# Two DeepNorm hybrid layers on one core: output projection in weight pieces of 512 columns, input projection in four chunks instead of six, modulation mostly in pieces of 512 features

## The chip, the cores and the metric

The kernel runs on one core of a Trainium2 chip. TensorE (PE) multiplies, VectorE (DVE), ScalarE (ACT) and GpSimd (POOL) do the elementwise work, and SyncE's queue (SP) issues all the transfers between HBM and SBUF. What is measured is the time of one execution on the device, in microseconds; a kernel's time is the median of its runs.

## The reference, cut to what matters

Two layers over 1024 latent tokens and 256 context tokens, 1024 features, all in float32. Each layer is

```python
mod = silu(c) @ ada_w + ada_b                     # 6 x 1024 features: shift, scale, gate, twice; modc from c_ctx
z = (x * (1 + sc1) + sh1) @ w_in                  # 1984 columns, split into:
q_lat, kv_lat, k_r, dq, dk, dv, zch               # 384, 256, 64, 256, 256, 256, 512
o_m = attention(q, k, v)                          # 4 heads from q_lat, kv_lat, k_r; rotary positions
o_d = attention(dq, dk, dv)                       # 4 heads of two maps each, the second subtracted; rotary positions
y = concat(o_m, rms_norm(o_d), chunk_mix(gelu(zch))) @ w_o
x = layer_norm(alpha * x + g1 * y)
x = layer_norm(alpha * x + g2 * conv_ffn(x * (1 + sc2) + sh2))
```

The context tokens go through the same with `modc`; they attend to the context alone, and in layer 1 only their keys and values are needed.

## The kernel before

Every product is made from float32r parts: a matrix is split into `hi` and `lo` (`split`, L455: a ScalarE copy and a subtraction by VectorE or GpSimd), and three matmuls per block of 128 features give `ah*bh + ah*bl + al*bh` (`mm3`, L437). All matmuls of `mm` have line L435. A tile of 128 tokens is the stationary operand, and the weights stream.

The program is written in order as tasks, each with the tiles that it reads and writes, and a planner (`Sched`) then issues them oldest first on a model of the engines, with a cost for each task; an `either` task goes to VectorE or GpSimd. The planner's order is fixed when the kernel is built; each engine, SP's queue too, runs its own list in that order. Places are limited: 8 banks for sums (tag `t`), regions of SBUF that hold the larger tiles (tag `S`, handed out in the program's order), 24 places of 512 words (`C`), 12 of 256 (`H`) and 12 of 512 for modulation weights (`M`).

A layer runs in five steps.

- **Input projection** (`in_proj`, `in_chunk`, `in_tile`). The 1984 columns are cut into six chunks, `ZCH`: z 512, dk 256, dv 256, dq 256, kv 320 (256 and the 64 of `k_r`), q 384. For each chunk the weights are loaded in pieces of up to 1280 words (8 blocks of features), split, and then all ten token tiles are multiplied, 24 matmuls a tile and chunk. Layer 1 takes the two context tiles in dk, dv and kv alone. Behind a tile of dk or dq, `post_d` (L917) rotates 256 columns with five VectorE products and a sum and stores them in `zd` in HBM; behind a tile of kv or q, `post_lat` (L857) normalizes, and `transpose_lat` (L887) transposes two tiles at a time (L901).
- **Attention** over 20 blocks of 256 queries (16 in layer 1). Between them stand the modulation pieces (`mod_piece`, L612) as fillers: 16 of layer 0 and 8 of layer 1 in layer 0, 16 in layer 1; eight more are made ahead of everything. A piece is 256 features: the four columns `s4` (both parts of two vectors) are stationary, 16 matmuls stream 256 columns each, `sel` joins the parts, and `fin` adds the bias.
- **Output projection** (`out_begin`, L1272; `out_half`, L1362). The weights come in 32 units of 256 columns, five to a piece of 1280 words, and are all held. A half tile, 512 features, is two groups of 24 matmuls of 256 columns in one bank. Ten tiles in layer 0, eight in layer 1; six of them stand ahead of the attention's last products (`EARLY`). Ahead of it `row_from_col` (L539) makes rows of the gate.
- **Feed-forward**, with 512-column matmuls for latent tokens and 256 for the context.
- **Norms**, and the transposed tokens for the next product (`emit_hT`, L672).

Of the kernel before, what the change touches and what calls it, by code (L numbers as in the profile page):

```python
# [20 lines left out]
P = 128  # L21
# [10 lines left out]
LAST = (2, 3)  # blocks of the hidden features whose down projection is left to the end, by layer  # L32
# attention: what a block of queries is made of, in this order (see attention)
# [3 lines left out]
COMB_END = 2  # blocks at the end whose two maps are joined by VectorE too  # L37
# [11 lines left out]
ZCH = ["z", "dk", "dv", "dq", "kv", "q"]  # L49
ZN = {"z": 512, "dk": 256, "dv": 256, "dq": 256, "kv": 320, "q": 384}  # L50
ZOFF = {"q": 0, "kv": 384, "dq": 704, "dk": 960, "dv": 1216, "z": 1472}
# [17 lines left out]
class Buf:  # L69
    """A tile that gets its place when its first task is issued."""  # L70
# [12 lines left out]
class Region:  # L83
    """A piece of SBUF that holds tiles of one type; it can change its type when it is empty."""
# [34 lines left out]
class Sched:  # L119
    """Issues a sequential program out of order, oldest task first, on a model of the engines.  # L120

    A task names what it reads and writes; what it depends on follows from the order in which the
    tasks are added. Places of tags in `fifo` are handed out in that order, so the program can
    always go on; no task starts more than `window` tasks ahead of the oldest open one."""
# [4 lines left out]
    def __init__(self, make, fifo, window):  # L129
# [7 lines left out]
        self.starved = None  # the task that waits for the next place of a tag in `fifo`  # L137
# [42 lines left out]
    def seat(self, b):  # L180
        """Gives b a place, or returns False."""
# [156 lines left out]
def either(n):  # L338
    return {**dve_t(n), **pool_t(n)}
# [1383 lines left out]
```

## Time and profile before

| | |
|---|---|
| median of 3 runs | 3498.62 us (3498.55 to 3498.67) |
| span of the profiled execution | 3494.7 us |
| TensorE busy | 3337.1 us, 95% |
| VectorE busy | 2528.8 us, 72% |
| ScalarE, GpSimd busy | 1390.8 us, 1103.9 us |
| matmuls | 19,658 |

The profiled execution has no time of its own beside its span, from the first to the last instruction; the median of the runs is 3.9 us above it. A row's "busy" is the time in which the engine worked on something of that row, and "idle before" the time in which it stood before those instructions, with what ended the wait. The input projection of layer 0 runs from about 82 to 286 us, its attention to about 819, its output projection to about 960; in layer 1 the three end at about 2122, 2604 and 2717 us.

### The profile page before, as it was taken

The page shows a single profiled execution, that of the slowest core. Times are in us where ns is not written, and L with a number is a line of the kernel's source. Part 1 is how long each engine was busy: PE and PEld are TensorE (multiplying, and loading weights), DVE is VectorE, ACT ScalarE, POOL GpSimd, SP SyncE. Part 2 cuts the span into 40 slices and gives each one's busy share as a digit, 9 for nine tenths or more (in the row PEclk, how much of TensorE's full clock was granted, in tenths as well). Part 3 has the DMA queues.
Part 4 walks back from the last instruction along what each step waited for, and adds up shares of the span by engine and source line. Part 5 has one row for each costly group of instructions (what it writes and reads, how often), then busy time and mean ns, then how long its engine had stood idle before and what let it go on. Part 6 is the DMA issues. An engine that isn't in the chain of part 4 may idle for free. (4 is left out here: it accounts for less than half of the span.)

```text
span 3494.7 us, 52898 instructions
## 1 busy us (share of the span) xinstructions
PE 3337.1 (95%) x19658; PEld 2916.4 (83%) x19658; DVE 2528.8 (72%) x6761; ACT 1390.8 (40%) x2428; POOL 1103.9 (32%) x665
## 2 busy tenths in 40 slices
PE   7999999998999999999997999999989899999997
PEld 6998888888988888888886898888879688888885
DVE  7467999998757656565679657999988755555557
ACT  5125666663442222222226225666653322222222
POOL 2102555542113311111134202444433433323322
PEclk9999999999999999999998999999999899999998
DMA  6212223223222211111114211222233311111111
GB/s 236 71 37 76 72 74 82 74 87 118 94 95 91 81 41 37 43 37 37 37 67 136 82 45 56 59 66 66 57 106 109 115 49 53 44 49 47 51 43 73
DMA packets 149258, 252.59 MB, mean 72 GB/s; under 512 B 53256, under 2 KB 85256, under 8 KB 149000
## 3 DMA queue, kind: packets, MB, share of 16 engines
q1 hardware_dynamic: 149000, 249.20, 22.1%
q8 instruction: 155, 2.54, 0.3%
q14 instruction: 103, 0.84, 0.1%
HBM read 209.04 MB, written 40.11 MB: 71 GB/s over the span
## 5 line engine op out<-in xcount | busy, mean ns | idle before, releaser
L435 PE MATMUL t<-region 128*128 128x256 f32 (+3 forms) x16336 | 3004.9, 343 | 77.9 <-DVE region L444 39.4
L435 PEld LDWEIGHTS t<-region 128*128 128x128 f32 x16336 | 2578.8, 191 | 440.3 <-DVE region L444 47.3
L444 POOL TENSOR_TENSOR region<-region 128x512 fp32r<-128x512 f32 (+6 forms) x393 | 620.5, 1586 | 1906.6 <-ACT region L447 1250.8
L1524 DVE SCALAR_TENSOR_TENSOR region<-t,conv,region 128x511 f32<-128x511 f32 (+2 forms) x616 | 341.6, 555 | 443.5 <-ACT region L1527 433.8
L1597 DVE TENSOR_TENSOR region<-region,t 128x512 f32<-128x512 f32 x760 | 456.3, 626 | 141.2 <-PE t L435 141.2
L447 ACT ACTIVATE region<-region 128x512 fp32r<-128x512 f32 (+4 forms) x502 | 385.8, 788 | 281.5 <-POOL region L1549 122.6
L1527 ACT ACTIVATE region<-t,conv 128x512 f32<-128x512 f32 (+1 forms) x220 | 161.4, 734 | 795.6 <-PE t L435 787.5
L447 ACT ACTIVATE region<-t 128x512 fp32r<-128x512 f32 (+4 forms) x711 | 321.4, 490 | 350.8 <-PE t L435 209.6
L444 DVE TENSOR_TENSOR region<-region 128x512 fp32r<-128x512 f32 (+7 forms) x361 | 333.8, 934 | 63.9 <-ACT region L447 52.8
L1099 DVE TENSOR_SCALAR_CACHE_REDUCE region<-t 128x512 f32<-128x512 f32 (+1 forms) x600 | 334.7, 585 | 11.6 <-PE t L435 9.5
L1104 ACT ACTIVATE region<-region,q 128x1280 f32<-128x1280 f32 (+1 forms) x216 | 273.5, 1267 | 162.6 <-DVE q L1103 148.4
L444 DVE TENSOR_TENSOR region<-t,region 128x512 fp32r<-128x512 f32 (+1 forms) x529 | 297.1, 597 | 33.7 <-ACT region L447 32.3
L1168 PE MATMUL t<-ident,region 128*128 128x128 f32 x1312 | 179.3, 280 | 19.2 <-DVE region L1141 8.2
L1144 POOL TENSOR_TENSOR region<-region 128x1280 f32<-128x1280 f32 (+1 forms) x68 | 185.5, 2728 | 5.7
L1168 PEld LDWEIGHTS t<-ident,region 128*128 128x128 f32 x1312 | 150.6, 144 | 27.5 <-DVE region L1141 8.6
L1143 POOL TENSOR_SCALAR region<-region,q 128x1280 f32<-128x1280 f32 (+1 forms) x68 | 85.7, 1261 | 228.5 <-DVE q L1138 104.3
L435 PE MATMUL t<-region,s 128*4 128x256 f32 x768 | 117.2, 292 | 12.9 <-ACT region L447 8.0
L1547 ACT ACTIVATE region<-region 128x512 f32<-128x512 f32 (+1 forms) x110 | 64.9, 590 | 150.0 <-DVE region L1524 149.9
L435 PEld LDWEIGHTS t<-region,s 128*4 128x4 f32 x768 | 64.9, 87 | 41.8 <-ACT region L447 8.2
L517 POOL TENSOR_TENSOR region<-region 128x1024 f32<-128x1024 f32 x31 | 76.0, 2461 | 74.9 <-ACT region L513 28.6
L924 DVE TENSOR_TENSOR region<-t,region 128x256 f32<-128x256 f32 x32 | 13.6, 425 | 110.3 <-PE t L435 110.2
L484 DVE SCALAR_TENSOR_TENSOR q<-q 128x1 f32<-128x1 f32 x276 | 82.2, 302 | 5.5
(127 smaller groups left out, 1758.5 us busy)
## 6 DMA issues: line engine op xcount, KB each, us to landing
region<-in_wup SPq DMA_DIRECT2D x88, 512.0 KB, 3.6
region<-in_ada_w SPq DMA_DIRECT2D x160, 256.0 KB, 3.0
region<-in_w_down SPq DMA_DIRECT2D x46, 512.0 KB, 3.7
n<-region SPq DMA_DIRECT2D x36, 512.0 KB, 2.9
region<-n SPq DMA_DIRECT2D x36, 512.0 KB, 4.4
region<-in_ada_w SPq DMA_DIRECT2D x16, 512.0 KB, 6.9
region<-in_w_o SPq DMA_DIRECT2D x12, 640.0 KB, 6.0
zd<-region SPq DMA_DIRECT2D x58, 128.0 KB, 1.7
```

The costliest lines, as they stand in the source:

```text
L435: self.nc.tensor.matmul(ps, a, b, start=start, stop=stop)
L444: eng.tensor_tensor(out=out, in0=full, in1=hi.bitcast(F32), op=ALU.subtract)
L447: self.nc.scalar.activation(out, in_, AF.Copy, **kw)
L484: self.task(t, lambda e: nc.vector.scalar_tensor_tensor(a.t, y.t, y.t, v.t, op0=ALU.mult, op1=ALU.mult), [y, v], [a])
L1099: self.task(dve_t(b - a), lambda e: nc.vector.tensor_scalar(p[:, a:b], ps[:, :b - a], -scale, None, op0=ALU.mult, op1=ALU.min, accum_out=n ...
L1104: self.task(act_t(nk, 0.19), lambda e: nc.scalar.activation(p[:, :nk], p[:, :nk], AF.Exp, bias=m.t, scale=-1.0, accum_out=s.t), [p, m], [p ...
L1143: nc.gpsimd.tensor_scalar(p2[:, :nk], p2[:, :nk], cc.t, 0.0, op0=ALU.mult, op1=ALU.add)
L1144: nc.gpsimd.tensor_tensor(out=p1[:, :nk], in0=p1[:, :nk], in1=p2[:, :nk], op=ALU.add)
L1168: nc.tensor.transpose(ps[:, u, j * P:(j + 1) * P], B[key][j][:, (kt + u) * P:(kt + u + 1) * P], self.ident)
L1524: nc.vector.scalar_tensor_tensor(o, i, x, o, op0=ALU.mult, op1=ALU.add)
L1527: self.task(act_t(n, 0.15), lambda e: nc.scalar.activation(t[:, a:b], u[:, :n], AF.Identity, scale=c[:, 1:2], bias=c[:, 3:4]), [u, "conv"] ...
L1597: self.task(dve_t(n), lambda e, b=b, o=o, c=c, n=n: nc.vector.tensor_tensor(out=b[:, o:o + n], in0=b[:, o:o + n], in1=ps[:, c:c + n], op=A ...
```

## The change

The six chunks of the input projection become four, z 512, d 512 (dk and dv together), kv 512 (256, the 64 of `k_r`, and 192 of dq) and q 448 (384, and the other 64 of dq, the queries of the last head). The two context tiles of layer 1 use only the first 320 columns of kv. `post_d` is called on a part of a bank: for dk on 256 columns, for dq once on 192 and once on 64, each with its five products, its sum and its store. A chunk's weights come in four pieces of 1024 words (896 for q).

The output weights come in 16 pieces of 512 columns (one block of features, one half), six loaded ahead in place of three pieces of 1280, and a half tile is one group of 24 matmuls of 512 columns.

A modulation piece in the attention has 512 features: eight slabs of 512 columns, 16 matmuls of 512 columns, a bank and a column tile of twice the size. There are 12 in layer 0 and 8 in layer 1. The eight pieces ahead of the program stay at 256 features. `prep_Q` reads dq by the part that holds its head. Comments are taken out too, so a line such as L435 is now L436.

```diff
-IN_AHEAD, FF_AHEAD, WO_AHEAD = 2, 1, 3
+IN_AHEAD, FF_AHEAD, WO_AHEAD = 2, 1, 6
...
-ZCH = ["z", "dk", "dv", "dq", "kv", "q"]
-ZN = {"z": 512, "dk": 256, "dv": 256, "dq": 256, "kv": 320, "q": 384}
...
+ZCH = ["z", "d", "kv", "q"]
+ZCOLS = {"z": [(1472, 1984)], "d": [(960, 1472)], "kv": [(384, 704), (704, 896)], "q": [(0, 384), (896, 960)]}
+ZN = {n: sum(b - a for a, b in c) for n, c in ZCOLS.items()}
...
+    def mod_piece(self, l, n, key=0):
+
+        j, h = QUADS[n // 2], n % 2
+        w = [self.weight(self.i["ada_w"][l, j, h, k], 512, self.M, key=key, acq=True) for k in range(KD)]
+        self.mod_part(l, j, 2 * h, 2, [x[0][0] for x in w], [x[1] for x in w], self.C(), key)
+
+    def mod_part(self, l, j, q, c, wk, wb, m4, key):
...
+        N = 256 * c
+        kk = KD // len(wb)
+        ps, pm = self.bank(), self.bank(F32, (P, 2 * c, 2))
+        for h in range(len(wb)):
             def go(e, h=h):
...
+                for k in range(kk * h, kk * (h + 1)):
+                    hi, lo = wk[k]()
+                    a = self.s4[:, k]
+                    self.mm(ps[:4, :N], a, hi, k == 0, False)
+                    self.mm(ps[:4, :N], a, lo, False, k == KD - 1)
+
+            self.task(mm_t(2 * kk, N), go, ["s4"] + wb[h], [ps], key=key, acq=[m4] if h == 0 else ())
...
     def in_tile(self, l, name, t, wk, wb, tabs):
         nc, hT, N = self.nc, self.hT, ZN[name]
+        dq = l == 0 or t >= 2
+        if name == "kv" and not dq:
+            N = 320
...
-                self.mm3(ps[:, :N], (a[0][:, cs], a[1][:, cs]), wk[k](), k == 0, k == KD - 1)
+                self.mm3(ps[:, :N], (a[0][:, cs], a[1][:, cs]), wk[k](0, N), k == 0, k == KD - 1)
...
-        elif name in ("dk", "dq"):
-            self.post_d(l, name, t, ps, dst, tabs["d"])
-        elif name == "dv":
...
+        elif name == "d":
+            dv = self.H()
+            self.post_d("dk", t, ps, 0, 256, 256, dst, tabs["d"])
+            self.task(act_t(256), lambda e: self.copy(dv.t, ps[:, 256:512]), [ps], [dv])
+            self.dma(lambda: self.zd[cs, 512:768], lambda: dv.t, 4 * P * 256, [dv], [("zd", "dv", t)])
         else:
+            a, n, off = (320, 192, 0) if name == "kv" else (384, 64, 192)
+            if dq:
+                self.post_d(f"dq{off}", t, ps, a, n, off, self.C() if n > 64 else self.H(), tabs["d"])
             return self.post_lat(l, name, t, ps, dst, tabs.get("k"))
...
-            self.task({"dve": 0.9}, rope, [ps, dtab], [o])
...
+            self.task({"dve": 0.55 + 1.4e-3 * n}, rope, [ps, dtab], [o])
...
-        units = [5] * 6 + [2]
-        wo = Stream(self, [dict(src=self.i["w_o"][l, j, :, :256 * n], n=256 * n, k=n) for j, n in enumerate(units)], WO_AHEAD)
-        wo.prime(3)
+        wo = Stream(self, [dict(src=self.i["w_o"][l, j], n=512) for j in range(2 * KD)], WO_AHEAD)
+        wo.prime(6)
...
-            for j in range(2):
-                for k in range(KD):
-                    self.mm3(ps[:, j * 256:(j + 1) * 256], y[k](), wk[4 * k + 2 * hh + j](), k == 0, k == KD - 1)
+            for k in range(KD):
+                self.mm3(ps.t, y[k](), wk[2 * k + hh](), k == 0, k == KD - 1)
...
-            ada = [(0, n) for n in range(8, 24)] + [(1, n) for n in range(8)] if l == 0 else [(1, n) for n in range(8, 24)]
+            ada = [(0, n) for n in range(4, 12)] + [(1, n) for n in range(4)] if l == 0 else [(1, n) for n in range(4, 12)]
```

Three places show how the order of the engines moves. A row has the line, the operation, the tiles, the output's shape and the number in a row. The first is TensorE at the end of the input projection of layer 0, before: matmuls of the q chunk (384 columns), the transposes of its results (L901), the queries' transposes of the attention (L1084), and the first modulation pieces (`s_70` is `s4`, `sel_71` is `sel4`).

```order
L435 MATMUL t<-region 128x384 x48
L901 MATMUL t<-ident,region 128x128 x6
L435 MATMUL t<-region 128x384 x48
L901 MATMUL t<-ident,region 128x128 x6
L1084 MATMUL t<-identr,region 128x128 x12
L435 MATMUL t<-region,s_70 4x256 x20
L435 MATMUL t<-sel_71,region 128x2 x2
L901 MATMUL t<-ident,region 128x128 x6
L435 MATMUL t<-region,s_70 4x256 x16
L435 MATMUL t<-sel_71,region 128x2 x2
```

And now, where the q chunk has 448 columns and the three lines are L914, L1098 and L436:

```order
L436 MATMUL t<-region 128x448 x72
L914 MATMUL t<-ident,region 128x128 x6
L436 MATMUL t<-region 128x448 x144
L914 MATMUL t<-ident,region 128x128 x18
L1098 MATMUL t<-identr,region 128x128 x8
L436 MATMUL t<-region,s_70 4x512 x10
L1098 MATMUL t<-identr,region 128x128 x4
L914 MATMUL t<-ident,region 128x128 x6
L436 MATMUL t<-region,s_70 4x512 x8
L436 MATMUL t<-sel_71,region 128x2 x4
```

The transposes that followed each two token tiles now stand in one run of 18 behind the last six tiles, with the queries' transposes and the first modulation products around the rest.

The second is SP's queue in the input projection of layer 0, before: the last loads of the weights of kv and q among the stores of the finished tiles (`yt` of chunk z, `zd` of dk, dv and dq).

```order
L432 DMA region<-in_w_in_q 128x1152
L432 DMA yt<-region 128x256
L432 DMA region<-in_w_in_q 128x1152
L432 DMA yt<-region 128x256
L432 DMA zd<-region 128x256
L432 DMA region<-in_ktab 128x1024
L432 DMA zd<-region 128x256 x2
L432 DMA yt<-region 128x256
L432 DMA zd<-region 128x256 x27
L432 DMA region<-in_w_in_q 128x768
```

And now, where a `zd` store of 256 columns is one of dk or dv, and one of 192 columns belongs to a tile of kv:

```order
L433 DMA region<-in_w_in_q 128x896 x2
L433 DMA zd<-region 128x256 x2
L433 DMA yt<-region 128x256
L433 DMA region<-in_ktab 128x1024
L433 DMA zd<-region 128x256 x2
L433 DMA yt<-region 128x256
L433 DMA zd<-region 128x256 x16
L433 DMA zd<-region 128x192 x2
L433 DMA region<-in_w_in_q 128x896
L433 DMA zd<-region 128x192
L433 DMA region<-in_w_in_q 128x896
L433 DMA zd<-region 128x192 x5
```

The last piece of q stood behind all of the stores of dq; now the last two stand behind the second and the third of the ten stores of the kv tiles.

The third is TensorE toward the end of layer 1's attention, before: the last modulation products, their `sel` product, and what follows; the transposes of the gate (L539) begin 13 rows behind that `sel` row.

```order
L435 MATMUL t<-region 128x256 x5
L1168 MATMUL t<-ident,region 128x128 x20
L435 MATMUL t<-region,s_70 4x256 x4
L435 MATMUL t<-region 128x512 x2
L435 MATMUL t<-region 128x256 x9
L435 MATMUL t<-region 128x512
L435 MATMUL t<-region 128x256 x4
L435 MATMUL t<-sel_71,region 128x2 x2
L1196 MATMUL t<-ident,q 128x128 x2
L435 MATMUL t<-region 128x256 x8
```

And now, the same place in the program, the last modulation piece, with L540 51 rows behind its `sel` row:

```order
L436 MATMUL t<-region,s_70 4x512 x2
L1182 MATMUL t<-ident,region 128x128 x4
L436 MATMUL t<-region 128x256 x12
L436 MATMUL t<-region,s_70 4x512 x4
L436 MATMUL t<-region 128x256 x4
L1182 MATMUL t<-ident,region 128x128 x4
L436 MATMUL t<-region 128x256 x4
L436 MATMUL t<-sel_71,region 128x2 x4
L1182 MATMUL t<-ident,region 128x128 x4
L436 MATMUL t<-sel_81,region 128x64 x2
```

The last modulation piece has moved ahead, away from the attention's last blocks.

## Rows read from the trace of the kernel before

**Rows 1.** The page's first lines: the span, and for each engine its busy time in us, its share of the span and its number of instructions.

```profile
span 3494.7 us, 52898 instructions
...
PE 3337.1 (95%) x19658; PEld 2916.4 (83%) x19658; DVE 2528.8 (72%) x6761; ACT 1390.8 (40%) x2428; POOL 1103.9 (32%) x665
```

**Rows 2.** Groups of TensorE's matmuls by line and shape, over the whole span: line, engine, operation, tiles, stationary operand and output, number; then busy us, mean ns of one (they overlap), and the idle time before them.

```profile
L435 PE MATMUL t<-region 128*128 128x512 f32 x8024 | 1922.5, 396 | 37.9 <-DVE region L444 17.4 <-ACT region L447 16.2 <-POOL region L444 2.2
L435 PE MATMUL t<-region 128*128 128x256 f32 x7256 | 979.4, 287 | 28.5 <-DVE region L444 22.0 <-DVE region L1099 3.8 <-DVE q L1103 0.8
...
L435 PE MATMUL t<-region,s 128*4 128x256 f32 x768 | 117.2, 292 | 12.9 <-ACT region L447 8.0 <-DVE region L444 4.7
L435 PE MATMUL t<-region 128*128 128x384 f32 x432 | 77.9, 338 | 0.0
L435 PE MATMUL t<-region 128*128 128x320 f32 x480 | 72.8, 310 | 0.0
```

**Rows 3.** Two stretches in which TensorE has matmuls of one width alone: 256 columns in the input projection of layer 0, and 512 in the feed-forward part of layer 1. Columns: from:to, us, then busy us (and number) of PE, PEld, DVE, ACT and POOL, the granted clock, the DMA share, GB/s.

```profile
130.00:180.00 50.00, 50.00 (x424) 50.00 (x423) 8.90 (x39) 4.22 (x11) 0.00 (x0) 1.00 0.15 48
...
2800.00:2900.00 100.00, 100.00 (x439) 82.08 (x438) 54.85 (x97) 25.48 (x33) 35.04 (x19) 1.00 0.14 47
```

**Rows 4.** The timeline of TensorE, merged: start us, length us, engine, line, operation, out<-in, number. In this order: modulation and the row after it, chunk z of the input projection, chunk kv, chunk q, and a token tile of the output projection; a stretch is read from its start to the start of the next row.

```profile
35.40 2.90 PE L435 MATMUL t<-region,s 128*4 128x256 f32 x24
38.23 0.60 PE L435 MATMUL t<-sel,region 4*128 4x2 f32 x4
...
41.40 8.47 PE L435 MATMUL t<-region 128*128 128x512 f32 x36
49.71 2.03 PE L435 MATMUL t<-region,s 128*4 128x256 f32 x16
...
221.67 7.27 PE L435 MATMUL t<-region 128*128 128x320 f32 x48
228.77 0.60 PE L901 MATMUL t<-ident,region 128*128 128x128 f32 x4
...
249.97 8.66 PE L435 MATMUL t<-region 128*128 128x384 f32 x48
258.47 0.82 PE L901 MATMUL t<-ident,region 128*128 128x128 f32 x6
...
833.65 11.76 PE L435 MATMUL t<-region 128*128 128x256 f32 x96
845.25 0.60 PE L1321 MATMUL t<-ident,region 128*128 128x128 f32 x4
```

**Rows 5.** Stretches, with the columns of rows 3: chunk kv and chunk q of layer 0, the end of the attention of layer 0, the output projection of layer 0 and of layer 1.

```profile
217.95:240.59 22.64, 22.64 (x161) 22.62 (x160) 20.70 (x123) 12.24 (x34) 2.73 (x1) 1.00 0.07 19
249.97:285.61 35.64, 35.64 (x213) 35.50 (x212) 23.75 (x117) 14.66 (x40) 2.29 (x3) 1.00 0.17 51
750.00:800.00 50.00, 41.31 (x292) 36.85 (x292) 47.22 (x120) 32.55 (x54) 15.97 (x8) 0.93 0.29 93
850.00:900.00 50.00, 50.00 (x421) 50.00 (x420) 41.17 (x169) 13.89 (x19) 3.87 (x3) 1.00 0.36 117
2650.00:2700.00 50.00, 50.00 (x421) 49.86 (x420) 44.86 (x150) 17.13 (x27) 15.52 (x8) 1.00 0.34 118
```

**Rows 6.** Groups of VectorE and ScalarE that follow the input projection, with the columns of rows 2: the rotation's products and sum (L924, L930, L933) in 124 to 217 us, the lower part of a q weight piece (218 to 241 us) and of a transposed block (250 to 286 us), and ScalarE's copies of weight pieces of 1024 and of transposed blocks over the whole span.

```profile
L930 DVE TENSOR_TENSOR region<-t,region 128x64 f32<-128x64 f32 x64 | 9.7, 215 | 0.0
L933 DVE TENSOR_TENSOR region<-region 128x256 f32<-128x256 f32 x15 | 6.4, 425 | 0.5
L924 DVE TENSOR_TENSOR region<-t,region 128x256 f32<-128x256 f32 x15 | 6.4, 425 | 58.0 <-PE t L435 58.0
...
L444 DVE TENSOR_TENSOR region<-region 128x1152 fp32r<-128x1152 f32 x1 | 1.4, 1353 | 0.0
...
L444 DVE TENSOR_TENSOR region<-t,region 128x256 fp32r<-128x256 f32 x11 | 4.0, 417 | 1.5 <-ACT region L447 1.5
...
L447 ACT ACTIVATE region<-region 128x1024 fp32r<-128x1024 f32 x158 | 162.0, 1049 | 29.6 <-PE t L435 8.8 <-DVE region L561 7.2 <-DMA region<-in_ada_w 4.7
L447 ACT ACTIVATE region<-t 128x256 fp32r<-128x256 f32 x193 | 67.1, 380 | 32.7 <-PE t L435 30.7 <-PE t L901 1.2
```

**Rows 7.** Groups of ScalarE and VectorE in 770 to 815 us, the end of layer 0's attention, with the columns of rows 2: both parts of the output weights in pieces of 1280, ScalarE's in pieces of 512, and VectorE's subtraction of 512 from a bank.

```profile
L447 ACT ACTIVATE region<-region 128x1280 fp32r<-128x1280 f32 x6 | 7.7, 1279 | 0.0
L447 ACT ACTIVATE region<-region 128x512 fp32r<-128x512 f32 x2 | 1.3, 627 | 0.3 <-PE t L435 0.3
...
L444 DVE TENSOR_TENSOR region<-t,region 128x512 fp32r<-128x512 f32 x18 | 11.7, 680 | 0.2
L444 DVE TENSOR_TENSOR region<-region 128x1280 fp32r<-128x1280 f32 x3 | 5.9, 1950 | 0.1
```

**Rows 8.** The page's DMA issues: out<-in, queue, operation, number, KB each, median us from issue to landing. The 16 loads of 512 KB are the first modulation pieces.

```profile
region<-in_ada_w SPq DMA_DIRECT2D x160, 256.0 KB, 3.0
...
region<-in_ada_w SPq DMA_DIRECT2D x16, 512.0 KB, 6.9
region<-in_w_o SPq DMA_DIRECT2D x12, 640.0 KB, 6.0
```

**Rows 9.** Waits of TensorE in 280 to 830 us, the attention of layer 0, the longest in total: who waits <- for whom, us in total, times, longest us.

```profile
PE t L435 <- DVE region L444: 13.6, 14, 2.4
PE t L1168 <- DVE region L1141: 4.3, 1, 4.3
```

More of the change, by code (lines that the diff above doesn't have):

```diff
@@ L606, in setup, with mod_load, mod_first @@
         self.n2 = d.tile([SEQ, D], F32, tag="n2", name="n2")
-    def mod_src(self, l, n, h):
-        return self.i["ada_w"][l, QUADS[n // 4], n % 4, h]
-    def mod_piece(self, l, n, key=0, raws=None):
+    def mod_load(self, n, h):
+        return self.load(self.i["ada_0"][QUADS[n // 4], n % 4, h], 1024, self.L)
+    def mod_first(self, n, raws):
+        w = [self.weight(None, 1024, self.L, k=4, raw=raws[h]) for h in range(2)]
+        self.mod_part(0, QUADS[n // 4], n % 4, 1, [f for x in w for f in x[0]], [x[1] for x in w], self.H(), 0)
@@ L613, in mod_piece @@
+    def mod_piece(self, l, n, key=0):
[3 more added lines that the diff above has]
+    def mod_part(self, l, j, q, c, wk, wb, m4, key):
         nc = self.nc
         self.s.what = f"mod{l}"
-        j, q = QUADS[n // 4], n % 4
-        if raws:
-            w = [self.weight(None, 1024, self.L, k=4, raw=raws[h]) for h in range(2)]
-        else:
-            src = [self.mod_src(l, n, h)[:, a:a + 512] for h in range(2) for a in (0, 512)]
-            w = [self.weight(x, 512, self.M, k=2, key=key, acq=True) for x in src]
@@ L634, in sel @@
+        self.task(act_t(N), lambda e: self.copy(m4[:4], ps[:4, :N]), [ps], [m4], key=key)
         def sel(e):
-            for k in range(2):
+            for k in range(2 * c):
                 self.mm(pm[:, k], m4[:4, k * P:(k + 1) * P], self.sel4)
-        self.task({"pe": 0.25}, sel, [m4, "sel4"], [pm], key=key)
-        ks = slice(2 * q, 2 * q + 2)
+        self.task({"pe": 0.25 * c}, sel, [m4, "sel4"], [pm], key=key)
+        ks = slice(2 * q, 2 * (q + c))
         o = self.modv[l][:, j, ks]
-        tok = ("modv", l, j, q)
@@ L643, in fin @@
         def fin(e):
[L644 removed]
+            nc.vector.tensor_tensor(out=o, in0=pm.t, in1=self.adab[l][:, j, ks].unsqueeze(2).to_broadcast([P, 2 * c, 2]), op=ALU.add)
             if j in (1, 4):
                 nc.vector.tensor_scalar(o, o, 1.0, None, op0=ALU.add)
[L648 removed]
+        self.task({"dve": 0.15}, fin, [pm, ("adab", l)], [("modv", l, j, q + x) for x in range(c)], key=key)
@@ L703, in mod @@
             for n in (q, 4 + q):
-                self.mod_piece(0, n, raws=[self.load(self.mod_src(0, n, h), 1024, self.L) for h in range(2)])
+                self.mod_first(n, [self.mod_load(n, h) for h in range(2)])
         mod(0)
@@ L805, in in_chunk @@
         held = []
-        tiles = range(0 if l == 0 or name in ("kv", "dk", "dv") else 2, NT)
+        tiles = range(0 if l == 0 or name in ("kv", "d") else 2, NT)
         for t in (8, 9, 0, 1) if l == 0 and name == "z" else tiles:
@@ L1273, in out_begin @@
         self.s.what = f"wo{l}"
-        units = [5] * 6 + [2]
-        wo = Stream(self, [dict(src=self.i["w_o"][l, j, :, :256 * n], n=256 * n, k=n) for j, n in enumerate(units)], WO_AHEAD)
-        wo.prime(3)
+        wo = Stream(self, [dict(src=self.i["w_o"][l, j], n=512) for j in range(2 * KD)], WO_AHEAD)
+        wo.prime(6)
         self.go = {s: self.row_from_col(lambda s=s: self.modv[l][:, 2, :, s], self.modtok(l, 2)) for s in ((0, 1) if l == 0 else (0,))}
-        w = [wo.get(j) for j in range(7)]
+        w = [wo.get(j) for j in range(2 * KD)]
         self.wo = [f for x in w for f in x[0]], [b for x in w for b in x[1]]
```

54 lines of the change are left out of this document (19 added, 35 removed).

## The prediction

> **What bounds the kernel now.** I read the page's busy shares first. TensorE works 3337.1 of 3494.7 us, VectorE 2528.8 [rows 1]: the time is TensorE's, and only what shortens its queue or fills its 158 us of gaps can count. Next, the matmuls by shape: 8,024 of 512 columns, 7,256 of 256, 768 of 256 for the modulation, 480 of 320, 432 of 384 [rows 2]. The mean durations there overlap, since matmuls are pipelined, so what one costs has to be read as a pitch: stretches with one shape and no gap, time divided by count. A stretch of 256 columns has 424 matmuls in 50.00 us, 117.9 ns each, and one of 512 columns 439 in 100.00 us, 227.8, both at a granted clock of 1.00 [rows 3]. The timeline of TensorE gives the rest as start-to-start differences [rows 4]: modulation 24 in 2.83 us (117.9), the 512-column chunk z 36 in 8.31 us (230.8), 320 columns 48 in 7.10 us (147.9), 384 columns 48 in 8.50 us (177.1), and 256 columns in the output projection 96 in 11.60 us (120.8). The granted clock of these stretches is the upper level, 2.4 GHz, at which 256 columns would stream in 106.7 ns and 512 in 213.3; so each matmul pays 11 to 17 ns beyond its columns. In the same windows the weight-load row is busy 50.00 of 50.00 us at 256 columns and 82.08 of 100.00 at 512 [rows 3]: at the narrow width loads leave no slack.
>
> **The change, part by part.** No column is added or taken away; the same columns go in fewer matmuls. The counts follow from the code: the input projection loses 48 of 120 per full token tile (18 tiles) and 24 of 72 on the two context tiles of layer 1, 912; the output projection loses 24 of 48 per half tile, 36 halves, 864; 40 modulation pieces become 20, and lose 320. Together 2,096.
>
> *Input projection.* Before, a full tile costs 24 x (3 x 117.9 + 147.9 + 177.1) = 24 x 678.7 ns. After, it is 24 x (512 + 512 + 448 columns). For 512 I take 229.4, the middle of 227.8 (feed-forward stretch) and 230.8 (the z chunk, the same operands' shape but with busy loads around it). No row has 448 columns; 384 costs 0.461 ns a column, 512 costs 0.445 to 0.451, so 199 to 207, and I take 204. That is 24 x 662.8, a gain of 0.38 us a tile, 6.9 for 18, and 0.3 for the two context tiles: **7.2 us**, bounds 4.8 (230.8 and 207) and 10.4 (227.8 and 199).
>
> *Output projection.* 48 x 120.8 = 5.80 us a half becomes 24 x 229.4 = 5.51: 0.29 us on 36 halves, **10.5 us**, bounds 9.3 and 11.8 by the two prices of 512. TensorE is busy throughout both stretches, and VectorE 41.17 and 44.86 of 50.00 us [rows 5]; with stages 5% shorter the second comes to about 95% and just keeps pace.
>
> *Modulation.* 2 x 117.9 - 229.4 = 6.4 ns on 320 matmuls, **2.0 us**; a stationary operand of four columns with 512 moving ones stands in no row, so bounds 0 and 5.
>
> *What is added.* The query columns of the differential heads lose their own chunk and are rotated from the banks of the kv and q chunks: two rotations of five VectorE operations for one, and two stores for one. They leave a stretch in which VectorE works 8.90 of 50.00 us [rows 3] for two in which it works 20.70 of 22.64 and 23.75 of 35.64 [rows 5]. One rotation of 256 columns takes 425 + 4 x 215 ns = 1.29 us [rows 6]; with that on top, VectorE needs at most 3.45 + 1.29 = 4.7 us for a kv tile that TensorE now works 5.5 us on, and 2.97 + 1.29 + 0.43 = 4.7 for a q tile of 4.9 plus transposes. Hidden, cost nothing, but with little room; if the cover went, up to 1.3 us on each of 34 tiles. The additional 18 stores go through SP's queue beside work that waits for nothing of theirs.
>
> *The end of the q chunk.* In the order, transposes that stood between the q tiles now stand in one run after the last tile, 18 in layer 0 and 12 in layer 1. Each pair is emptied by a ScalarE copy (380 ns) and a VectorE subtraction (417 ns) [rows 6], slower than TensorE fills them, six transposes in 0.82 us [rows 4]. Nine pairs: 3.8 us against 2.5. I put **2 us lost** for both layers, bounds 0 and 6.
>
> *Output weights.* Sixteen pieces of 512 in place of six of 1280 and one of 512: on ScalarE 16 x 0.63 = 10.0 us for 6 x 1.28 + 0.63 = 8.3, on VectorE 16 x 0.68 = 10.9 for 6 x 1.95 + 0.68 = 12.4 [rows 7]. These lie at the end of the attention, where TensorE waits for VectorE (41.31 against 47.22 of 50.00 us busy [rows 5]), so they count: between -1.5 and +1.7 us a layer, taken as 0. Loads shrink from 640 KB (6.0 us to landing) towards the 256 KB that take 3.0 [rows 8], and six are ahead in place of three: as many bytes, nothing on the path. The modulation's loads stay 160 of 256 KB, with one slab, not two, for each wait of TensorE on a pair of hi and lo parts, and the same number of waits.
>
> *Sum.* 7.2 + 10.5 + 2.0 - 2.0 = 17.7 us. 3494.7 - 17.7 = 3477.0 for the span; the runs' median, 3498.6, lies 3.9 us above the profiled span, so **3481 us**. Its own range, with the bounds not all at one end, is 3472 to 3490.
>
> **The rivals.**
> A. *Width is worth almost nothing.* Per column, 256, 320 and 384 cost 0.461, 0.462 and 0.461 ns [rows 3, 4]: a price by the column, not by the matmul. If the new 512s went by it (236 ns), the input projection and the modulation would gain nothing and the output projection 36 x (5.80 - 24 x 0.236) = 4.8 us: 3494, within 0.2%. The two rows that do have 512 columns (227.8 and 230.8) speak against it, and one of them has the same operands. The Trainium skill comes to the same side in another way (TensorE: Matmul & The Clock Gate, "Back-to-back issue gap"): it gives a gap of N/2.4 + 2.5 ns, so halving the count would save only 2.5 ns a matmul, 5 us in all and about 3493, an estimate by that page. The trace disagrees with its floor: 117.9 ns stand where it has 109.2, and 227.8 to 230.8 where it has 215.8.
>
> B. *The ends of the attention get shorter too.* TensorE waits 13.6 us on VectorE's subtractions in layer 0's attention and after [rows 9], most at its end. In the order of TensorE the last modulation product of layer 1 now stands 51 rows before the first transpose of the residual gate in place of 13, and in layer 0 35 in place of 13, so four or more splits of 0.63 and 0.68 us leave that end. If 5 us a layer go with them: 3471.
>
> C. *Slower: a chunk waits for its weights.* A chunk's weights are now four pieces that must all be there for its first tile, and a load stands behind others in SP's queue and waits for a place that TensorE's earlier chunk gives up. If the last piece is issued later than landing plus splits before its first use, 6.9 us [rows 8] + 1.05 + 1.35 [rows 6] = 9.3 us, TensorE stands for up to that at each of six switches (three in each layer). From three such stalls on (28 us against 17.7) the change loses: 3509. Against it: in the order the last two q loads of layer 0 stand behind two and three of the ten stores of the kv tiles, some seven tiles, 38 us, ahead of use.
>
> **How the numbers follow.** Forecast 0.60; A 0.15; B 0.11; C 0.10; 0.04 for gains that are spread over new small waits, near 3495. Differences under 0.2%, 7 us, are about what a measurement of this kernel cannot tell from none. Faster by more is nearly all of the forecast and B, 0.70; within 0.2% is A, the last case and the forecast's weak end, 0.20; slower is C, 0.10. The range takes in B's 3471 with the bounds' best sum below it, and A, but not C: 3468 to 3497.
>
> **What would show it.** In the profile after: 17,562 matmuls in place of 19,658; a half of the output projection in 5.5 us, 24 at about 229 ns; a run of 512 columns in the d chunk at the same pitch and 448 near 204. C would show as TensorE's gaps ended by ScalarE or VectorE splits of pieces of 1024 at the start of d, kv or q; A as a pitch of 236; a gap of over 5 us behind the last q tile would upset the 2 us there. The forecast fails if VectorE's share in the kv or q chunk reaches its whole and the tile time is then set by it.

## The result, and the profile after

The changed kernel takes 3535.47 us (median of 4 runs, 3535.01 to 3539.42) against 3498.64: a ratio of 1.0109, 95% interval 1.0095 to 1.0123. The forecast was 3481 us. The profiled execution took 3535.01 us with a span of 3533.2. Every ratio in this document is of runs in the chip's faster state; the one run outside it, of e11, took 6577.16 us. First the head of the page of the changed kernel:

```profile
span 3533.2 us, 48850 instructions
...
PE 3343.4 (95%) x17562; PEld 2798.8 (79%) x17562; DVE 2541.3 (72%) x6859; ACT 1386.1 (39%) x2421; POOL 1080.3 (31%) x668
```

The change does what it says: 17,562 matmuls. But TensorE is busy 6.3 us more than in [rows 1] with 2,096 fewer, and 32.2 us longer without work. The timeline of TensorE (columns of rows 4) gives the new pitches: in chunk kv, chunk q, the modulation and a token tile of the output projection.

```profile
205.65 11.14 PE L436 MATMUL t<-region 128*128 128x512 f32 x48
216.63 0.64 PE L914 MATMUL t<-ident,region 128*128 128x128 f32 x4
...
259.80 15.37 PE L436 MATMUL t<-region 128*128 128x448 f32 x74
275.00 1.69 PE L914 MATMUL t<-ident,region 128*128 128x128 f32 x14
...
302.51 2.48 PE L436 MATMUL t<-region,s 128*4 128x512 f32 x10
304.83 1.22 PE L436 MATMUL t<-region 128*128 128x256 f32 x9
...
847.97 11.26 PE L436 MATMUL t<-region 128*128 128x512 f32 x48
859.07 0.60 PE L1334 MATMUL t<-ident,region 128*128 128x128 f32 x4
```

48 in 10.98 us are 228.8 ns (forecast 229.4); 74 in 15.20 are 205.4 (204); 10 in 2.32 are 232; 48 in 11.10 are 231.3. The prices of the sum stand (the last is 0.5 ns above its upper bound), so the loss is elsewhere. Nine stretches show where, with the columns of rows 3 (the second is the length): up to the last product of layer 0's q chunk; from there to the first transposes of probabilities (the junction below); the rest of the attention; output projection; feed-forward; norm and input projection of layer 1 up to its last q product; its attention; its output projection; the rest. The kernel before:

```profile
0.00:285.80 285.80, 264.37 (x1730) 243.83 (x1731) 181.29 (x680) 93.42 (x179) 45.14 (x33) 0.96 0.33 110
285.80:323.40 37.60, 35.88 (x273) 31.16 (x272) 26.01 (x86) 22.16 (x60) 3.22 (x5) 0.95 0.35 104
323.40:819.50 496.10, 466.25 (x3336) 415.24 (x3337) 458.85 (x1379) 330.40 (x643) 251.83 (x161) 0.98 0.27 78
819.50:960.60 141.10, 139.15 (x1127) 136.50 (x1126) 109.86 (x412) 52.79 (x83) 25.32 (x24) 0.99 0.33 107
960.60:1810.60 850.00, 849.98 (x4194) 718.32 (x4193) 528.56 (x922) 230.20 (x344) 177.63 (x94) 1.00 0.16 54
1810.60:2118.20 307.60, 282.96 (x1766) 260.66 (x1765) 227.62 (x848) 109.26 (x210) 85.20 (x62) 0.94 0.27 87
2118.20:2610.50 492.30, 454.62 (x3196) 405.75 (x3195) 443.08 (x1298) 309.20 (x581) 213.26 (x125) 0.97 0.23 69
2610.50:2729.10 118.60, 117.38 (x916) 113.46 (x915) 101.14 (x326) 40.86 (x65) 39.13 (x27) 0.99 0.37 123
2729.10:3494.70 765.60, 726.54 (x3137) 591.54 (x3135) 452.41 (x815) 202.48 (x267) 263.17 (x135) 0.97 0.16 55
```

And the changed kernel:

```profile
0.00:275.20 275.20, 256.79 (x1238) 211.88 (x1239) 175.19 (x702) 92.35 (x176) 46.25 (x41) 0.98 0.33 113
275.20:322.00 46.80, 42.09 (x276) 33.71 (x275) 32.14 (x109) 26.35 (x69) 11.71 (x14) 0.93 0.34 94
322.00:834.10 512.10, 469.87 (x3155) 405.90 (x3154) 468.44 (x1378) 324.76 (x632) 228.91 (x146) 0.97 0.26 75
834.10:986.00 151.90, 138.77 (x647) 113.33 (x645) 110.14 (x415) 52.44 (x83) 22.82 (x22) 0.94 0.30 99
986.00:1842.90 856.90, 856.58 (x4194) 717.61 (x4193) 530.35 (x923) 230.25 (x344) 175.49 (x93) 1.00 0.16 54
1842.90:2156.10 313.20, 282.38 (x1332) 237.02 (x1331) 228.26 (x882) 109.30 (x208) 86.16 (x67) 0.94 0.26 84
2156.10:2644.00 487.90, 452.09 (x3069) 395.03 (x3067) 440.58 (x1311) 307.60 (x578) 209.68 (x127) 0.98 0.25 70
2644.00:2764.90 120.90, 115.20 (x532) 94.49 (x531) 104.38 (x333) 40.85 (x65) 35.40 (x22) 0.96 0.35 120
2764.90:3533.20 768.30, 729.63 (x3137) 589.84 (x3135) 451.77 (x814) 202.18 (x267) 263.88 (x136) 0.97 0.16 55
```

After less before, in this order: -10.6, +9.2, +16.0, +10.8, +6.9, +5.6, -4.4, +2.3, +2.7 us, together 38.5. Three things are to be seen. Layer 0's projection gains more than forecast, and its junction gives nearly all of it back. Some of this is work that changed sides. TensorE's modulation products and transposes of q in the junction, before and then in the changed kernel (columns of rows 2):

```profile
L435 PE MATMUL t<-region,s 128*4 128x256 f32 x48 | 7.6, 318 | 1.5 <-ACT region L447 1.1 <-DVE region L444 0.4
L901 PE MATMUL t<-ident,region 128*128 128x128 f32 x12 | 1.8, 282 | 0.0
```

```profile
L436 PE MATMUL t<-region,s 128*4 128x512 f32 x32 | 9.2, 397 | 2.5 <-DVE region L445 1.8 <-ACT region L448 0.7
L914 PE MATMUL t<-ident,region 128*128 128x128 f32 x24 | 3.3, 278 | 0.3 <-DVE region L445 0.3
```

Twelve transposes have left the stretch ahead of the last q product and stand here, 1.6 us at six in 0.82 us, and 32 modulation products at 232 ns take 1.8 us more than 48 at 118: together some 3.4 of the 9.2 us, an estimate. The rest is 3.0 us more without work for TensorE (4.7, 1.7) and a lower granted clock (0.93, 0.95). Up to the end of the junction the changed kernel is 1.4 us ahead. The rest of the attention loses 16.0 although VectorE and GpSimd together are given about the same work: some of it has moved from GpSimd (251.83 to 228.91) to VectorE (458.85 to 468.44). And the two feed-forward stretches, which the change doesn't touch (4,194 and 3,137 matmuls in both), are 9.6 us longer.

The waits of TensorE (columns of rows 9) in the rest of the attention, and in layer 0's output projection:

```profile
PE t L436 <- DVE region L445: 28.0, 26, 3.4
...
PE t L679 <- ACT region L514: 9.8, 1, 9.8
```

In [rows 9], over a somewhat longer stretch, the first was 13.6. The second is one wait of the transposes behind a norm; windows around it (columns of rows 3) show what follows a wait:

```profile
935.00:940.00 5.00, 0.71 (x6) 0.47 (x4) 4.73 (x15) 1.02 (x2) 1.51 (x2) 1.00 0.01 2
940.00:945.00 5.00, 0.00 (x0) 0.00 (x0) 2.25 (x14) 2.03 (x3) 0.00 (x0) 0.59 0.00 0
945.00:950.00 5.00, 4.32 (x19) 3.92 (x19) 3.26 (x9) 4.37 (x10) 1.50 (x3) 0.50 0.68 212
950.00:955.00 5.00, 3.06 (x6) 1.99 (x7) 4.97 (x11) 1.46 (x3) 1.55 (x2) 0.50 0.85 312
955.00:960.00 5.00, 5.00 (x17) 3.96 (x16) 2.71 (x14) 0.00 (x0) 0.00 (x0) 0.71 0.00 0
```

The granted clock falls to the lower level, 1.2 GHz (0.50), and TensorE is at work again for some ten microseconds before it is back: this wait is paid twice.

### The profile page after: what moved, and what is told of

The parts are those of the page before. It is cut to its first block, busy times and chain, and to the rows that moved or that the text cites. A ratio compares the mean times of both kernels' runs of the same rounds, so it can differ in the third digit from the quotient of the medians.

```text
span 3533.2 us, 48850 instructions
## 1 busy us (share of the span) xinstructions
PE 3343.4 (95%) x17562; PEld 2798.8 (79%) x17562; DVE 2541.3 (72%) x6859; ACT 1386.1 (39%) x2421; POOL 1080.3 (31%) x668
## 5 line engine op out<-in xcount | busy, mean ns | idle before, releaser
L436 PE MATMUL t<-region 128*128 128x512 f32 (+4 forms) x14560 | 2999.9, 364 | 84.8 <-DVE region L445 49.2
L436 PEld LDWEIGHTS t<-region 128*128 128x128 f32 x14560 | 2478.6, 190 | 557.5 <-DVE region L445 61.7
L445 POOL TENSOR_TENSOR region<-region 128x512 fp32r<-128x512 f32 (+4 forms) x376 | 579.1, 1548 | 1787.5 <-ACT region L448 1276.4
L448 ACT ACTIVATE region<-region 128x512 fp32r<-128x512 f32 (+3 forms) x522 | 387.7, 765 | 296.6 <-POOL region L1561 121.8
L448 ACT ACTIVATE region<-t 128x512 fp32r<-128x512 f32 (+5 forms) x684 | 313.1, 499 | 354.7 <-PE t L436 193.4
L445 DVE TENSOR_TENSOR region<-region 128x512 fp32r<-128x512 f32 (+5 forms) x398 | 354.5, 902 | 74.9 <-ACT region L448 55.4
L436 PE MATMUL t<-region,s 128*4 128x512 f32 (+1 forms) x448 | 118.9, 381 | 23.3 <-DVE region L445 12.7
L937 DVE TENSOR_TENSOR region<-t,region 128x256 f32<-128x256 f32 (+2 forms) x48 | 16.1, 336 | 116.4 <-ACT region L448 70.3
L448 ACT ACTIVATE region<-t,q 128x64 f32<-128x64 f32 (+2 forms) x110 | 38.9, 384 | 121.4 <-DVE q L487 110.6
```

The source lines that it names most:

```text
L436: self.nc.tensor.matmul(ps, a, b, start=start, stop=stop)
L445: eng.tensor_tensor(out=out, in0=full, in1=hi.bitcast(F32), op=ALU.subtract)
L448: self.nc.scalar.activation(out, in_, AF.Copy, **kw)
```

## The experiments

Ratios are against the kernel before, run on the same chip.

**One part each** (e1, e2, e3). The hunks of the change for one part alone, in the kernel before:

```diff
-ZCH = ["z", "dk", "dv", "dq", "kv", "q"]                       # e1, with in_tile, post_d, prep_Q
+ZCH = ["z", "d", "kv", "q"]
-        wo = Stream(self, [... 256 * n ... for j, n in enumerate(units)], WO_AHEAD)   # e2, with out_half
+        wo = Stream(self, [dict(src=self.i["w_o"][l, j], n=512) for j in range(2 * KD)], WO_AHEAD)
-    def mod_piece(self, l, n, key=0, raws=None):               # e3, with mod_part and the list ada
+    def mod_piece(self, l, n, key=0):
```

> The kernel before with the input projection in four chunks and nothing else. If the losses belong to the parts that they stand at, this one keeps the gain of layer 0's projection (10.6 us from the first to the last product of the q chunk in the changed kernel), loses about 5 us in the stretch from layer 0's last norm to layer 1's q chunk, and leaves the attention at its time of before: about 3493 us. If any new order of the planner shifts the attention and the ends of the stages, whatever was edited, the attention of layer 0 moves by some 10 to 25 us here too, in either direction, and the total is between 3485 and 3515.

> The kernel before with the output projection in 16 weight pieces of 512 columns and nothing else. If the pieces are the loss (16 pieces of 512 words, two to a region of 1280, hold more places than six of 1280 and one of 512, so loads of the last token tiles come late), the wait of some 10 us for a norm in layer 0's output projection and its drop of the granted clock stand here too, and the time is 3508 to 3515. If the pieces are harmless, the 10.5 us of the prediction show: 3488.

> The kernel before with the modulation of the attention in pieces of 512 features and nothing else. If half as many and twice as long fillers are what costs layer 0's attention its 25 us, the time is about 3520. If they are harmless, 2 us are gained: 3497. If only the shuffled order counts, the attention of both layers moves by 5 to 25 us in either direction.

Measured: e1 3530.62 us, 1.0092 (1.0075 to 1.0108), above what either of its theories allowed; e2 3512.91, 1.0044 (1.0029 to 1.0059); e3 3527.40, 1.0086 (1.0071 to 1.0101). Each part alone loses, together 80 us (before: 3496.96), more than twice what all three lose at once: these can't all be costs that belong to the parts. e3 alone could be read by its theory of the fillers as well as by that of the order; e7 and e8 below decide. e2 has the time that its first theory asked for, but not its wait: layer 0's output projection takes 144.2 us (141.1 before); 6.2 us are in the untouched feed-forward of layer 0, and one wait of 18.0 us for a GpSimd subtraction stands behind layer 1's output projection. The rest of layer 0's attention takes 515.5 us in e3, and in e1:

```profile
320.20:839.70 519.50, 478.23 (x3336) 424.12 (x3337) 466.57 (x1373) 333.41 (x645) 257.54 (x166) 0.96 0.25 75
```

e1 has the same matmuls in this stretch as the kernel before (3,336), and takes 23.4 us longer in it.

**Width alone** (e4). The pieces of before, and so its tasks and its order; only the matmuls are wider:

```diff
-            for j in range(2):
-                for k in range(KD):
-                    self.mm3(ps[:, j * 256:(j + 1) * 256], y[k](), wk[4 * k + 2 * hh + j](), k == 0, k == KD - 1)
+            for k in range(KD):
+                u = 4 * k + 2 * hh
+                if u % 5 < 4:
+                    self.mm3(ps.t, y[k](), wk[u](0, 512), k == 0, k == KD - 1)
+                else:
+                    for j in range(2):
+                        self.mm3(ps[:, j * 256:(j + 1) * 256], y[k](), wk[u + j](), False, False)
```

> The kernel before with its weight pieces of 1280 columns as they are, but matmuls of 512 columns wherever both units of 256 lie in one piece, 13 of 16 of each token tile; tasks, costs, places and loads are those of before, so the planner's order is too. This is the width alone: 864 x 13/16 = 702 matmuls less, 13/16 of 10.5 us gained: 3490. If width is worth almost nothing in the whole, because VectorE or the norms set the pace, 3497 to 3499.

Measured: 3492.56 us, 0.9985 (0.9976 to 0.9995): 4.4 us less (medians), about half of what the prices give. Its two output projections (columns of rows 3; 141.10 and 118.60 us before):

```profile
817.90:955.10 137.20, 133.68 (x736) 114.07 (x735) 109.33 (x413) 52.69 (x83) 25.50 (x24) 1.00 0.33 110
...
2608.40:2726.80 118.40, 114.86 (x605) 96.66 (x604) 101.31 (x326) 40.80 (x65) 39.10 (x27) 0.98 0.36 123
```

Layer 0 gains 3.9, layer 1 nothing: there TensorE works 2.5 us less and stands 2.3 us longer. Of its waits in that stretch 2.2 us are for ScalarE's splits and 0.6 for VectorE's, and VectorE works as long as before (101.31 us, 101.14); which of the two engines holds the stage isn't shown.

**Places** (e5, e6). In the program as built, a matmul's operands lie at one of three offsets within 256 bytes (0, 192 and 224 before, 32, 192 and 224 in the changed kernel), by when a region's first tile came. With these addresses laid beside the trace, 512-column matmuls whose operands and next weights share the offset have another pitch than the others:

```
                 same offset        other
before        6051 at 228.0    1745 at 233.1 ns
after         5131 at 229.0    4397 at 232.9 ns
```

The edit, in the kernel before (e5) and the changed one (e6), moves every large tile to one offset, 224, and leaves each engine's instructions and their order as they were:

```diff
         self.s = Sched(make, ("S",), WINDOW)
+        for r in self.s.regions:
+            sb.tile([P, r.words], F32, tag=r.name, name="region", bufs=1)
```

> The kernel before, all 32 regions claimed at the start, one behind the other, so that every operand of a matmul lies at the same offset of 256 bytes; tasks, order and loads are those of before. In the trace of before 512-column matmuls whose two operands and next weights share that offset have a pitch of 228.0 ns, the others 233.1; 1745 are of the other kind. If the place in memory sets the pitch, they fall to 228 or under, the stretch 2800 to 2900 us has 440 or more matmuls in place of 439, and the time is 3484 to 3492. If the pitch has another cause, 3497 to 3499.

> The changed kernel with its regions claimed in the same way. 4397 of its 512-column matmuls are of the other kind, at 232.9 ns. If places set the pitch, some 25 to 30 us go, most of it in the two feed-forward stretches, the projections and the attention: 3505 to 3512. If not, 3535.

Measured: e5 3488.87 us, 0.9974 (0.9964 to 0.9984); e6 3513.03, 1.0035 (1.0023 to 1.0047), where the change had 1.0109, a little above what was expected. 2900 to 3000 us, feed-forward of layer 1, 512 columns alone (columns of rows 3): the kernel before, the changed one, e5, e6.

```profile
2900.00:3000.00 100.00, 100.00 (x438) 81.98 (x437) 54.16 (x94) 25.90 (x34) 35.07 (x19) 1.00 0.14 48
```

```profile
2900.00:3000.00 100.00, 100.00 (x435) 81.21 (x434) 53.87 (x94) 25.48 (x33) 34.61 (x19) 1.00 0.15 48
```

```profile
2900.00:3000.00 100.00, 100.00 (x443) 82.81 (x442) 55.73 (x97) 25.85 (x34) 35.66 (x19) 1.00 0.14 48
```

```profile
2900.00:3000.00 100.00, 100.00 (x443) 82.81 (x442) 55.74 (x98) 26.13 (x34) 36.44 (x20) 1.00 0.14 48
```

438, 435, 443 and 443 matmuls: 228.3, 229.9 and twice 225.7 ns, at one clock and with one work. The two feed-forward stretches, 850.0 and 765.6 us before and 856.9 and 768.3 in the changed kernel, take 844.5 and 759.2 in e5 and 845.1 and 757.1 in e6: with places alike nothing of their 9.6 us is left. Places change the pitch, the change had more tiles in unlike places, and that is 0.74% of its time (1.0109 to 1.0035) against 0.26% before: some 17 us of its loss, with an interval of about 0.1% to either side on each of the ratios. The Trainium skill (SBUF — State Buffer, "Who interferes with whom") gives TensorE two independent read ports, for the moving operand and for the weights. That gives no reason for places to matter, and e5 and e6 show that they do. That the offset, and not another property of a place, does it rests on the two classes above, since e5 moved every large tile.

**The same work in another order** (e7, e8). The kernel of e5 with one constant of the planner changed:

```diff
-def dve_t(n, per=1.042e-3, extra=0.0):     # e7
+def dve_t(n, per=1.05e-3, extra=0.0):
-MODKEY = 120                               # e8
+MODKEY = 110
```

> The kernel of e5 with nothing changed but a constant in the planner's model: VectorE's cost of 1.042 ns an element becomes 1.05. The work is the same, instruction for instruction; the order moves from the end of the input projection on. If the kernel's order is one that any reshuffle makes worse, layer 0's attention gets 10 to 25 us longer, with more waits and a lower granted clock, and the time is 10 to 35 us above e5. If losses come from what the edits themselves do (more splits, larger pieces, fewer fillers), it is within 5 us of e5.

> The kernel of e5 with nothing changed but MODKEY, 120 to 110: how far ahead of its place in the program the planner may take a modulation piece. Same work; the order moves in the attentions alone. By the theory of the reshuffled order 5 to 30 us above e5 with the loss in the attentions and behind them; by the theory of the edits' own costs within 5 us of e5.

Measured: e7 3514.72 us, 1.0048 (1.0030 to 1.0066), 25.9 above e5; e8 3510.21, 1.0031 (1.0019 to 1.0042), 21.3 above. The rest of layer 0's attention in e5, e7 and e8:

```profile
324.80:823.80 499.00, 469.46 (x3335) 418.91 (x3336) 458.22 (x1378) 330.68 (x643) 251.84 (x161) 0.98 0.26 77
```

```profile
324.30:845.50 521.20, 477.46 (x3329) 426.99 (x3330) 470.80 (x1381) 331.57 (x646) 243.02 (x155) 0.95 0.25 75
```

```profile
322.00:836.20 514.20, 474.78 (x3330) 422.93 (x3331) 468.23 (x1395) 328.85 (x638) 244.56 (x154) 0.96 0.25 75
```

All three have the same matmuls and the same transfers, in another order. With no edit of the work the stretch gets 15 to 22 us longer, in the way of the changed kernel: `either` tasks go from GpSimd to VectorE, TensorE waits for VectorE's subtractions 27.6 us in e7 (12.8 in e5), and the clock is lower. e8 also loses 11.4 us in layer 0's output projection (152.5 us), as the change did.

**The change's edits in the old order** (e9). Input projection of e1, width of e4, places of e5; from the attention's set-up to layer 1's input projection, and from layer 1's set-up on, a task is issued only when it is its engine's next in the list that the planner made for the kernel before:

```diff
+                    if t.at is not None and (t.at[2] != e or t.at[1] > low[t.at[0]] + (loose or 0) or loose < 500 and mine[t.at[0], e][head[t.at[0], e]] is not t):
+                        skipped.append(x)
+                        continue
```

> Regions claimed at the start as in e5, input projection in four chunks, output projection with matmuls of 512 on the old pieces as in e4, modulation as before; and from the attention's set-up on, in both layers, every engine runs its tasks in the order that the planner made for the kernel before (that order is read from a list; 28 of 2938 tasks of TensorE stand elsewhere, for want of a place). If the losses of e1 came from the reshuffled order, layer 0's projection keeps its gain of 10 to 15 us, its attention takes 532 to 542 us in place of 563, and the time is 3465 to 3475. If they came from the four chunks themselves (two rotations for one, more stores, transposes in a run), the attention stays at 550 or more and the time at 3490 or more.

Measured: 3497.11 us, 1.0004 (0.9995 to 1.0014): 22 to 32 us above what the first theory asked for, and where the second, a cost of the four chunks themselves, put it. The stretches don't all say so. The junction, the rest of the attention, and layer 1's output projection:

```profile
272.50:321.50 49.00, 40.13 (x287) 33.95 (x285) 32.26 (x105) 26.02 (x69) 5.07 (x7) 0.86 0.33 95
321.50:819.00 497.50, 464.79 (x3335) 414.05 (x3336) 458.16 (x1377) 329.76 (x643) 252.83 (x162) 0.99 0.26 78
...
2607.20:2736.40 129.20, 116.50 (x604) 96.47 (x603) 101.04 (x328) 41.02 (x65) 39.58 (x27) 0.95 0.34 118
```

The rest is back at 497.5 us, with VectorE's and GpSimd's shares of before: the loss there was the order's. But the junction takes 49.0 us, 11.3 more than in e5, 1.6 of them for the twelve transposes that moved into it. The four chunks alone don't set this. The junction of e1 and of e12 (below), both with four chunks and the old modulation, and of e7, with six:

```profile
276.80:320.20 43.40, 39.10 (x286) 33.29 (x285) 29.65 (x99) 23.86 (x66) 9.15 (x11) 0.92 0.32 97
```

```profile
275.00:314.80 39.80, 35.21 (x263) 30.76 (x262) 29.57 (x96) 22.24 (x59) 7.34 (x8) 0.96 0.41 111
```

```profile
281.60:324.30 42.70, 38.63 (x280) 33.40 (x277) 28.53 (x93) 22.89 (x62) 5.40 (x8) 0.92 0.34 92
```

The longest wait of e9's junction stands in its timeline:

```profile
272.38 1.69 PE L939 MATMUL t<-ident,region 128*128 128x128 f32 x14
...
281.44 1.33 PE L939 MATMUL t<-ident,region 128*128 128x128 f32 x5 [6.13 <-ACT region L479]
```

Behind the last q product only transposes of earlier tiles are left, and then TensorE waits for the last tile's norm (6.13 us) at the attention's head: ScalarE begins on that tile 2.9 us behind its last product, behind nine copies, and VectorE's small steps of the norm have three subtractions of some 0.7 us among them. The granted clock of the stretch is 0.86. How much of the 11.3 us is the chunks' and how much that of a list made for six chunks stays open. The 10.7 us in layer 1's output projection hold one wait of 8.2 us for a ScalarE split; whether the list or the chunks make it stays open.

**Gains added, and fresh draws** (e10, e11, e12). e10 is e4 with the places of e5. A draw is here one of the many orders that the planner makes of the same work when its constants are changed. e11 is e6, the whole change, with other constants, which gave the best of some twenty orders by the planner's own clock; e12 is e10 with e1's chunks and a draw of its own (the constants are put into one line each):

```diff
-MODKEY, SLACK, EARLY, FILL_END = 120, 150, (4, 2), 2                                 # e11
+MODKEY, SLACK, EARLY, FILL_END = 80, 200, (5, 1), 1
-MODKEY, WINDOW, SLACK, AHEAD, EARLY, FILL_END = 120, 450, 150, 300, (4, 2), 2        # e12
+MODKEY, WINDOW, SLACK, AHEAD, EARLY, FILL_END = 130, 420, 180, 250, (5, 1), 1
```

> e4 and e5 together: the order of before, regions claimed at the start, output projection with matmuls of 512 on the old pieces. The two gains lie in different places and should add: 4.4 and 10.4 us below before, 3483 to 3486. If the widths only filled time in which TensorE then waits, 3489.

> The changed kernel of e6 with other constants of the planner (MODKEY 80, SLACK 200, EARLY (5, 1), FILL_END 1, the best of some twenty drawings by the planner's own clock); its work is that of the change. By the theory of the order the losses of e6 are a bad draw and 10 to 25 us go, in layer 0's attention and output projection: 3488 to 3503. By the theory of the edits' own costs it stays near 3513.

> e9 without the list: input projection in four chunks, output projection as in e4, regions claimed at the start, and constants of the planner drawn in the same way (MODKEY 130, WINDOW 420, SLACK 180, AHEAD 250, EARLY (5, 1), FILL_END 1). By the theory of the order a fresh draw, some 5 to 20 us above e9: 3475 to 3492. If the four chunks cost the attention by themselves: 3505 or more.

Measured: e10 3481.44 us, 0.9959 (0.9945 to 0.9974), the two gains multiplied (0.9985 x 0.9974 = 0.9959), a little below what was expected, and the fastest here. e11 3489.32 (median of eight runs, 3481.65 to 3497.10), 0.9976 (0.9966 to 0.9986): the matmuls and transfers of the change in another order, by the ratios some 21 us faster than e6, and faster than before. e12 3494.17, 0.9992 (0.9983 to 1.0002), just outside what was expected. The rest of the attention and the output projection in e11:

```profile
321.10:824.80 503.70, 467.00 (x3154) 404.10 (x3153) 468.80 (x1371) 327.76 (x636) 232.83 (x147) 0.98 0.26 77
824.80:962.40 137.60, 132.80 (x647) 109.52 (x646) 108.78 (x414) 52.41 (x83) 24.36 (x23) 1.00 0.33 110
```

503.7 and 137.6 us with pieces, widths and fillers of the change: what it lost there (512.1 and 151.9; 511.5 and 151.5 in e6) was for the most part a draw. In the total no run shows the gains that were forecast for the input projection and the modulation: with places alike the change in e11 (0.9976) stands where the kernel before does in e5 (0.9974), and e12 (0.9992) lies above e10 (0.9959), although its junction ends 9.7 us earlier (314.8 us, 324.5).

## Why the prediction was wrong

**The step that failed** is one that was not in the sum: that a change of the work leaves all else as it is. The text took each part's cost against the trace of before, as if the attention, which no term but the modulation and the output weights touched, and the feed-forward part kept their times. It had no term for the order and none for the places. The planner's order is a function of every task's cost and of the places that are free, and the order of before is a good draw: the six kernels that keep it in the rest of layer 0's attention (e2 but for the output weights) take 494.5 to 499.0 us there, and the eight with another order 503.7 to 521.2. A new order alone, with no change of the work, cost 21 to 26 us (e7, e8), against a forecast gain of 17.7: TensorE waited 28.0 us for VectorE's subtractions in that stretch of the changed kernel, and 13.6 before in the longer one of [rows 9]. The forecast saw the orders move and read them for waits one by one (the q loads, the last `sel`), not for this.

**The account of +38.5 us**, against -17.7: by places some 17 us more than before (e5, e6), which hold the feed-forward's 9.6; by the order, the output projection of layer 0 (10.8, gone in e11) and the rest of the attention (16.0, less what of it is places; 7.6 are left in e11); in the junction 9.2, of which some 3.4 are work that moved in, and of which no run tells the chunks' own part from the order's. Against these stand the gains. The parts overlap, so this is no closed sum.

**The terms.** *Input projection*, 7.2: the pitches were right (228.8 and 205.4), and layer 0 gained 10.6 up to its last q product, more than its share of ten tiles. Of the rest 1.6 us are the twelve transposes that now stand behind that product, and TensorE stood 21.4 us ahead of it and now 18.4, at a granted clock of 0.96 and now 0.98. In layer 1 the same stretch, with the norm ahead of it, got 5.6 us longer: transposes in and behind the kv chunk wait 2.5 and 3.4 us there; with the work of the change in e11 it takes 305.5 us, 2.1 less than before. The bounds of this term come to 4.6 and 10.8 by its own prices, not 4.8 and 10.4, and 32 tiles are rotated in parts, not 34; neither touches the forecast. *The end of the q chunk* was mis-sized for the order that was built: 2 us for both layers, bounds 0 and 6, and in layer 0 alone the junction grew by 9.2 (8.0 between e5 and e6, 37.7 us and 45.7), some 6 of them beyond the work that moved in. The step counted how fast the transposes are emptied, not the last tile's norm that the run ends in, nor the clock behind the wait. *Output projection*, 10.5: nearly right in layer 0 as far as e4 shows (3.9 us, where 13/16 of 20 halves at 0.29 are 4.7; 2.4 between e5 and e10), nothing in layer 1: there "just keeps pace" did not hold, since TensorE waited for what it saved. *Modulation*, 2.0: 232 ns are within its bounds; no run isolates it, since e3 changes the order. *Output weights* at 0: not isolated either, but e11 has them and no loss in the stretch behind them.

**The rivals.** A, width worth nothing: refuted by the pitches and e4. B, shorter ends of the attention: refuted in layer 0, whose stretch got 16.0 us longer, and in layer 1 4.4 us came of its 5. Of the 13.6 us of waits that B builds on, only 6.0 lie behind 700 us, where the text has "most". C, slower by chunks that wait for their weights: the right side for a wrong reason; TensorE waits for no split at the start of d, kv or q, and its time up to the last q product of layer 0 fell.

## What to carry to other kernels

Where a planner makes the order, run the kernel before with a constant changed that alters no work, before a few tenths of a per cent are credited to an edit: here that alone costs 21 to 26 us, and the tuned order is a part of the kernel that an edit throws away. So judge an edit over several draws, or with the old order held (as in e4, and e9 with care). And claim a kernel's large tiles at the start, so that their places don't depend on the order: 10 us for two lines.

## What the runs showed of the hardware

The pitch of a 512-column float32r matmul changes with where its operands lie in SBUF: 225.7 ns in 2900 to 3000 us where all share an offset within 256 bytes (e5, e6), 228.3 and 229.9 in the kernels where some don't, at a granted clock of 1.00 in each; by the two classes, 228.0 and 233.1 in the trace of before. And behind a wait of 9.8 us the granted clock was 0.50 for some ten microseconds of work (the windows above).
